# A decoder layer on one core: weight sums of the down projection made by an accumulating DMA, and one more chunk with seven products

## The chip, the core and the metric

The kernel runs on one core of one Trainium2 chip. TensorE (PE in the profile) multiplies, VectorE (DVE) and ScalarE (ACT) do elementwise work, GpSimd (POOL) little here, and SyncE (SP) issues nearly all DMAs. The time is device microseconds of one execution; the median of the runs shown is 377.06 us (376.8 to 377.14, three runs). The profile is of one more execution, which took 376.66 us; its span, from the first to the last instruction, is 374.9 us, and 1.8 us lie around it. All arithmetic is in float32. TensorE takes float32 at full pace only in a rounded form (fp32r), so each operand is split into a rounded part `hi` and a remainder `lo`, and each product is three matmuls: hi x hi, lo x hi, hi x lo.

## The reference

A decoder layer on 256 tokens of width 1024: a mixer with pooled windows and attention, a cross attention into 256 memory tokens, and a feed-forward block, each followed by a layer norm. The change touches the last product of the last block only:

```python
def swiglu(h, w_gate, w_up, w_down):
    return (jax.nn.silu(h @ w_gate) * (h @ w_up)) @ w_down
...
h = layer_norm(DEEPNORM_ALPHA * h + swiglu(h, w_gate[l], w_up[l], w_down[l]),
               ln3_g[l], ln3_b[l])
```

`w_down` is 2816 x 1024. The activations that it multiplies are 256 x 2816.

## The kernel before

**Tiles of weights.** All weights run through one `Stream`, as tiles of 128 rows and 512 KB, in the order of use. A tile goes three ways: a DMA on SyncE's queue brings it from HBM into a raw buffer, which the profile calls w103r for tile 103 (there are `RAW_BUFS` = 7 of them); ScalarE casts it to w103h; VectorE subtracts to get w103l. `prepare` issues the cast and the subtraction, up to ten tiles ahead of TensorE (`W_BUFS` + `LATE_BUFS`), and `fetch_ahead` (L112) issues loads as raw buffers come free. Each queue runs in the order in which the program wrote it, so a load that waits for a raw buffer holds back the loads behind it.

**Chunks.** The feed-forward width 2816 is cut into eleven chunks of 256. Gate and up make the activations of chunk after chunk (tiles up to w102); for each, `Gated` adds two parts of the product (L963, L964), applies the activation (L968, L969) and splits the result (L429, L430). Then down multiplies chunk by chunk, in the order `DOWN` (L38).

**Eight products, or seven.** A chunk's part of down is a 2 x 2 block matrix (128 inputs of the chunk by 512 outputs) times a 2 x 2 block matrix of activations (two token halves of 128). `eight` (L1054) does it with eight block products of 128 x 512, 24 matmuls. `seven` (L1033) does it in the Strassen-Winograd way with seven, 21 matmuls, into the eight PSUM banks m[0] to m[7]; it pays with sums of activation blocks (L977 to L984, with a second split at L984) and of weight blocks. Seven chunks, 1 to 7, go through `seven`; chunk 0 goes third through `eight`; the last three chunks (`LAST`: 8, 9, 10) go through `pieces`, which ends quarter by quarter so that the last norm can begin.

**A pair.** In `seven`, the chunk's two weight tiles are x = (x1, x2) and y = (y1, y2), each half 512 wide. `prepare_pair` (L122) makes four sums in three steps, all on VectorE, and needs a third raw buffer, z:

- step 0: z1 = x2 - x1 (L135), z2 = y2 - x2 (L136), the remainder of x1, called the corner residual (L137, tile w103c), x2 := y2 - z1 (L138), the remainder of y (L139);
- step 1: x1 := y1 - x2 (L142), the remainder of z (L143);
- step 2: the remainder of x, which now holds two sums (L146).

So a pair takes three tile numbers: 103, 104 and 105 are x, y and z of the first. ScalarE's casts (L133, L134, L141, L145) run beside. TensorE takes three products after step 0 (the corner's and two of y's tile), two after step 1 and two after step 2. Before the change tiles 103 to 108 are the first two pairs (chunks 1, 2), 109 and 110 the plain tiles of chunk 0, 111 to 125 the other five pairs, 126 to 131 the plain tiles of `LAST`. z is never loaded.

**The end.** When the pairs are through, VectorE forms the sums of the banks (u2, u3) and the residuals (L1111 to L1121), and the two token halves go through the last norm. Its power (L725) runs on GpSimd, and for the first half so does the last add (L742).

Of the kernel before, what the change touches and what calls it, by code (L numbers as in the profile page):

```python
# [11 lines left out]
OP = mybir.AluOpType  # L12
# [3 lines left out]
D = 1024  # L16
# [18 lines left out]
BUSY = 7  # L35


DOWN = (1, 2, 0, 3, 4, 5, 6, 7, 8, 9, 10)  # L38
SEVEN = (1, 2, 3, 4, 5, 6, 7)
LAST = DOWN[-3:]  # L40
ALL = slice(None)

# [3 lines left out]
def r32(t):  # L46
    return t.bitcast(F32)


class Stream:  # L50
# [38 lines left out]
    def fetch(self, upto, queue):  # L89

        while len(self.raws) < min(upto, len(self.src)):
            i = len(self.raws)
            for load in self.loads.pop(i, []):
                load()
            src = self.src[i]
            if i < len(self.homes):
                raw = self.homes[i]
            else:
                raw = self.raw_pool.tile(self.shape(i), F32, tag="raw", name=f"w{i}r")
            if src is not None:  # L100
                for s, q in self.cuts.get(i, [(slice(None), queue)]):
                    q.dma_start(raw[:, :, s], src[:, :, s])
            self.raws.append(raw)

    def shape(self, i):
# [16 lines left out]
    def prepare_pair(self, i, hi, lo):  # L122
        nc = self.nc
        first, step = self.pairs[i]
        self.fetch(first + 3, nc.sync)
        x, y, z = self.raws[first:first + 3]
        h = x.shape[2] // 2
        (x1, x2), (y1, y2), (z1, z2) = [(a[:, :, :h], a[:, :, h:]) for a in (x, y, z)]
        sub = nc.vector.tensor_sub

        if step == 0:
            own = self.corner[first] = self.own(first)
            nc.scalar.copy(own[:, 0:1, :], x1)  # L133
            nc.scalar.copy(hi, y)  # L134
            sub(z1, x2, x1)  # L135
            sub(z2, y2, x2)  # L136
            sub(own[:, 1:2, :], x1, r32(own[:, 0:1, :]))  # L137
            sub(x2, y2, z1)  # L138
            sub(lo, y, r32(hi))  # L139
        elif step == 1:  # L140
            nc.scalar.copy(hi, z)  # L141
            sub(x1, y1, x2)  # L142
            sub(lo, z, r32(hi))  # L143
        else:
            nc.scalar.copy(hi, x)  # L145
            sub(lo, x, r32(hi))  # L146
# [60 lines left out]
def decoder_layer(  # L207
# [3 lines left out]
    nc = tc.nc  # L211
# [17 lines left out]
    def accbank(name):  # L229
        return pa.tile([P, 512], F32, tag="acc", name=name)  # L230


    ws = Stream(nc, rp, wp)
# [30 lines left out]
    c_dn = {}  # L264
    for c in DOWN:
        tiles = [w_down[k * P:(k + 1) * P, :].rearrange("(k p) n -> p k n", p=P) for k in (2 * c, 2 * c + 1)]
        c_dn[c] = ws.add_pair(*tiles) if c in SEVEN else [ws.add(w, 1)[0] for w in tiles]
    ws.own = lambda i: sp.tile([P, 2, 512], F32R, tag="pair", bufs=3, name=f"w{i}c")
# [3 lines left out]
    class Both:  # L272
# [9 lines left out]
        def pair(self, k, ts=ALL):  # L282
            t, j = self.tiles[k // 4], k % 4
            return t[:, j, 0, ts], t[:, j, 1, ts]
# [17 lines left out]
    def split_xt(k, n=2):  # L302
        split(*xT.parts(k, n), xr[:, k:k + n, :])
# [7 lines left out]
    def split_mem(k):  # L311
        split(*mT.parts(k, 4), mr[0][:, k:k + 4, :])
# [46 lines left out]
    def three(ps, w, y, start, stop, part=False):  # L359

        (wa, wb), (ya, yb) = w, y
        nc.tensor.matmul(ps, wa, ya, start=start, stop=False, skip_group_check=part)  # L362
        nc.tensor.matmul(ps, wa, yb, start=False, stop=False, skip_group_check=part)  # L363
        nc.tensor.matmul(ps, wb, ya, start=False, stop=stop, skip_group_check=part)  # L364
# [63 lines left out]
    def split(h, l, ps):  # L428
        nc.scalar.copy(h, ps)  # L429
        nc.vector.tensor_sub(l, ps, r32(h))  # L430
# [5 lines left out]
    def transpose_tok(dst, tok, t, k0):  # L436

        ps = bank("tp")
        for k in range(4):
            nc.tensor.transpose(ps[:, k * P:(k + 1) * P], tok[:, (k0 + k) * P:(k0 + k + 1) * P], ident)  # L440
        ts = slice(t * P, (t + 1) * P)
        split(*dst.parts(k0, 4, ts), ps.rearrange("p (k t) -> p k t", k=4))
# [145 lines left out]
    sums = {}  # L588
# [109 lines left out]
    class Norm:  # L698
# [9 lines left out]
        def add(self, c0, c1, acc):  # L708
            self.sum(c0, c1, acc)
            self.measure(c0, c1)  # L710
# [201 lines left out]
    def gated_parts(c):  # L912


        if c in SEVEN:
            t = ap.tile([P, 2, 8, P], F32R, tag="a8", name=f"g{c}")
            gT[c] = t[:, 0], t[:, 1]
            return
        i, j = divmod([c for c in sorted(DOWN) if c not in SEVEN].index(c), 2)
        if i == 0 and j == 0:  # L920
            shared[i] = ap.tile([P, 2, 8, P], F32R, tag="a8", name=f"go{i}")
        if i == 0:
            gT[c] = tuple(shared[i][:, n, 4 * j:4 * j + 4] for n in range(2))
        elif j == 0:
            gT[c] = tuple(sp.tile([P, 4, P], F32R, name=f"go{n}", tag="pr", bufs=PR_BUFS) for n in range(2))
        else:
            t = ap.tile([P, 2, 4, P], F32R, tag="a8", name=f"go{i}")
            gT[c] = t[:, 0], t[:, 1]

    def gated_pair(c, k, t):  # L930

        return pair(gT[c], ALL, 2 * k + t)
# [18 lines left out]
    class Gated:  # L951
# [19 lines left out]
        def split(self):  # L971
            gated_parts(self.c)
            hi, lo = gT[self.c]
            q = self.sums[0].rearrange("p f (t s) -> p (f t) s", t=T)
            split(hi[:, 0:4], lo[:, 0:4], q)
            if self.c in SEVEN:
                a11, a21, a12, a22 = [q[:, i] for i in range(4)]  # L977
                sums = sp.tile([P, 4, P], F32, name="sg", tag="pr", bufs=PR_BUFS)
                s1, s2, s3, s4 = [sums[:, i] for i in range(4)]
                nc.vector.tensor_add(s1, a21, a22)  # L980
                nc.vector.tensor_sub(s3, a11, a21)
                nc.vector.tensor_sub(s2, s1, a11)
                nc.vector.tensor_sub(s4, a12, s2)  # L983
                split(hi[:, 4:8], lo[:, 4:8], sums)  # L984

    first = [bank("pg") for t in range(T)]
# [37 lines left out]
    m = {n: accbank(f"m{n}") for n in (1, 2, 3, 5)}  # L1024
# [3 lines left out]
    def into(n, y, w, cols=ALL, ps=None):  # L1028

        three((m[n] if ps is None else ps)[:, cols], y, w, n not in begun, True, True)  # L1030
        begun.add(n)

    def seven(c):  # L1033


        first = c_dn[c][0]
        plan = (((1, 0, None), (2, 2, 0), (3, 7, 1)), ((5, 4, 0), (7, 6, 1)), ((6, 5, 1), (4, 3, 0)))
        for i, products in enumerate(plan):
            ws.prepare(first + i + 1)
            hi, lo = ws.tiles[first + i]  # L1040
            for n, form, half in products:
                if half is None:
                    own = ws.corner[first]
                    w = own[:, 0], own[:, 1]
                else:
                    w = tuple(a[:, 0, half * 512:(half + 1) * 512] for a in (hi, lo))
                into(n, pair(gT[c], ALL, form), w)
                yield
            ws.used += 1
            ws.next()  # L1050

    QUARTERS = {2: (0, 0, 512), 3: (0, 512, D), 4: (1, 0, 512), 0: (1, 512, D)}

    def eight(c):  # L1054

        for k, number in enumerate(c_dn[c]):
            ws.prepare(number + 1)
            hi, lo = ws.tiles[number]
            for n, (t, c0, c1) in QUARTERS.items():
                into(n, gated_pair(c, k, t), (hi[:, 0, c0:c1], lo[:, 0, c0:c1]))  # L1060
            ws.used += 1
            ws.next()
            yield

    def pieces():


# [18 lines left out]

    def down():
        for c in DOWN[:-len(LAST)]:
            yield from (seven if c in SEVEN else eight)(c)

    dn = down()
    run(dn, 2)
    left.multiply()
# [5 lines left out]
    lower, upper = slice(0, 512), slice(512, D)  # L1099
    norms = [Norm(3, t, h2[:, t, :]) for t in range(T)]  # L1100

    def with_residual(t, s, y):
        nc.vector.scalar_tensor_tensor(norms[t].r[:, s], h2[:, t, s], ALPHA, y, op0=OP.mult, op1=OP.add)
# [4 lines left out]
    def shared_sum(name):  # L1108
        return sp.tile([P, 512], F32, name=name, tag="pr", bufs=PR_BUFS)

    m1, u2, u3 = [shared_sum(name) for name in ("m1", "u2", "u3")]  # L1111
# [3 lines left out]
    with_residual(0, upper, m[5])  # L1115
    nc.vector.tensor_add(u3, m[7], u2)
    with_residual(1, upper, m[5])
    nc.vector.tensor_add(norms[0].r[:, upper], norms[0].r[:, upper], u2)
    nc.vector.tensor_add(norms[1].r[:, upper], norms[1].r[:, upper], u3)
    with_residual(1, lower, u3)  # L1120
    add(norms[1], 768, D, m[0][:, 256:])  # L1121
    rest = [sp.tile([P, CW], F32R, name=f"rest{i}", tag="pr", bufs=PR_BUFS) for i in range(2)]
    nc.scalar.copy(rest[0], norms[1].r[:, 768:])
    dn = pieces()
# [87 lines left out]
```

## Time and profile before

| | |
|---|---|
| median of the runs | 377.06 us |
| the profiled execution, its span | 376.66 us, 374.9 us |
| TensorE, weight loads | 368.5 us (98%), 317.6 us (85%) |
| VectorE, ScalarE, GpSimd | 306.8 us (82%), 204.1 us (54%), 19.6 us (5%) |
| DMA, mean over the span | 71.93 MB, 192 GB/s |
| granted TensorE clock | 0.997 |
| down, from its first matmul to TensorE's last long wait | 312.3 to about 367 us |

In a row of a timeline the first number is the start in us from the span's start, the second the length in us, then engine, source line, operation, `out<-in` by the names of the tiles, and the number of instructions merged in the row. Matmuls overlap in the pipeline: the distance of their starts is what one costs. VectorE's instructions overlap a little as well (0.69 us long, 0.60 apart), so distances of starts are used there too. In brackets stands the idle time before an instruction and what ended it. In the list of DMA issues the last number is the time from issue to landing in us. The down stage is where tiles 103 and up are used; VectorE works on them from 288.83 us on, some 20 us ahead.

### The profile page before, as it was taken

What the parts mean: (1) busy time and instruction counts of PE and PEld (TensorE: products, weight loads), DVE (VectorE), ACT (ScalarE), POOL (GpSimd) and SP (SyncE); (2) the same over time, 40 slices, a digit from 0 to 9 for tenths busy, and PEclk for the clock granted to TensorE, in tenths of its full rate; (3) what the DMA queues carried; (4) which work ended last, traced back from release to release, by engine and by line L of the source; (5) the groups of instructions that cost most, each with busy time, mean ns of one, the idle gap of its engine ahead of it and who ended that gap; (6) DMA issues with size and microseconds to landing.
All of it is one profiled execution on the core that took longest, in us unless ns stands there. A gap on an engine that the chain in (4) does not pass through costs nothing.

```text
span 374.9 us, 5582 instructions
## 1 busy us (share of the span) xinstructions
PE 368.5 (98%) x2061; PEld 317.6 (85%) x2061; DVE 306.8 (82%) x498; ACT 204.1 (54%) x330; POOL 19.6 (5%) x27
## 2 busy tenths in 40 slices
PE   9999999999999999999999999999999999999994
PEld 8997878787888889998888888888898888888883
DVE  6768799975599677865889688888888999999984
ACT  6746677644154635644237675567665675546510
POOL 1000033400020000000100000000000000000021
PEclk9999999999999999999999999999999999999998
DMA  8997784668508963343106958665554453375202
GB/s 274 415 416 270 222 282 124 214 214 292 169 0 281 387 210 133 113 156 123 60 2 221 326 184 278 226 219 176 173 180 170 152 170 113 119 275 162 64 0 112
DMA packets 20891, 71.93 MB, mean 192 GB/s; under 512 B 2304, under 2 KB 3072, under 8 KB 20736
## 3 DMA queue, kind: packets, MB, share of 16 engines
q1 hardware_dynamic: 20432, 71.12, 54.3%
q10 hardware_dynamic: 432, 0.46, 0.4%
q8 instruction: 16, 0.26, 0.3%
q14 instruction: 11, 0.09, 0.1%
HBM read 70.52 MB, written 1.05 MB: 191 GB/s over the span
## 4 chain that ended last, share of the span: by engine, by line
PE 97%; DMA 1%; DVE 1%; ACT 0%; issue 0%; POOLq 0%; ACTq 0%
PE pg L377 19%; PE pg L383 10%; PE pqk L483 6%; PE m L362 5%; PE m L364 5%; PE m L363 5%; PE acc L362 4%; PE acc L363 4%; PE acc L364 4%; PE pxk L377 4%; PE pxq L377 4%; PE pxq L383 2%; PE pu L377 2%; PE pxk L383 2%; PE xv L362 2%; PE xv L364 2%
## 5 line engine op out<-in xcount | busy, mean ns | idle before, releaser
L725 POOL TENSOR_TENSOR rs<-rs,mhalf 128x1 f32<-128x1 f32 x6 | 5.0, 830 | 291.2 <-DVE rs L724 291.2
L429 ACT CAST g<-sg 128x512 fp32r<-128x512 f32 x14 | 8.7, 621 | 19.1 <-DVE sg L983 12.4
L430 DVE TENSOR_TENSOR g<-sg,g 128x512 fp32r<-128x512 f32 x14 | 9.7, 692 | 8.9 <-ACT g L429 8.9
L964 DVE TENSOR_TENSOR sg<-pg,sg 128x256 f32<-128x256 f32 x40 | 14.1, 416 | 0.0
L963 ACT COPY sg<-pg 128x256 f32<-128x256 f32 x40 | 11.8, 379 | 2.1 <-PE pg L383 2.1
L968 ACT ACTIVATE sg<-sg 128x512 f32<-128x512 f32 x10 | 6.3, 635 | 12.1 <-DVE sg L964 12.0
L520 ACT ACTIVATE xpr<-xs,mx 128x256 f32<-128x256 f32 x8 | 3.7, 470 | 14.3 <-DVE mx L531 14.3
L520 ACT ACTIVATE pr<-pr,mx 128x128 f32<-128x128 f32 (+1 forms) x16 | 7.1, 445 | 7.6 <-DVE mx L551 7.6
L429 ACT CAST h2T<-tp 128x512 fp32r<-128x512 f32 x4 | 2.3, 586 | 12.9 <-PE tp L440 12.9
L730 DVE SCALAR_TENSOR_TENSOR r<-r,mv,gb 128x512 f32<-128x512 f32 (+2 forms) x12 | 8.3, 722 | 0.0
L717 DVE BATCH_NORM_STATS2 st<-r 128x6 f32<-128x512 f32 (+1 forms) x12 | 8.0, 670 | 0.3
L969 DVE TENSOR_TENSOR sg<-sg 128x512 f32<-128x512 f32 x10 | 6.9, 692 | 0.8
L596 POOL TENSOR_TENSOR win<-upad 128x542 f32<-128x542 f32 x2 | 4.0, 1998 | 56.9 <-DVE upad L627 56.9
L525 DVE RECIPROCAL sm<-sm 128x2 f32<-128x2 f32 x12 | 2.0, 166 | 6.0 <-ACT xpr L520 4.5
L835 PE MATMUL xs<-xkTh,xq 128*128 128x256 f32 x32 | 6.4, 282 | 0.0
L429 ACT CAST h1T<-tp 128x512 fp32r<-128x512 f32 x4 | 2.4, 588 | 7.2 <-PE tp L440 7.2
L735 DVE SCALAR_TENSOR_TENSOR h<-r,rs,gb 128x512 f32<-128x512 f32 x8 | 5.7, 746 | 0.1
L596 POOL TENSOR_TENSOR win<-win 128x269 f32<-128x269 f32 (+3 forms) x4 | 5.8, 1446 | 0.2
L635 ACT CAST xkTh<-pxk 128x256 fp32r<-128x256 f32 x8 | 2.6, 377 | 5.5 <-PE pxk L383 5.5
L637 DVE TENSOR_TENSOR xkl<-pxk,xkTh 128x256 f32<-128x256 f32 x8 | 3.0, 416 | 3.1 <-ACT xkTh L635 3.1
L835 PEld LDWEIGHTS xs<-xkTh,xq 128*128 128x128 f32 x32 | 5.2, 190 | 0.2
L170 ACT CAST w39h<-w39r 128x1024 fp32r<-128x1024 f32 x1 | 1.0, 1049 | 7.8 <-PE acc L364 7.8
(1157 smaller groups left out, 1294.8 us busy)
## 6 DMA issues: line engine op xcount, KB each, us to landing
gb<-in_ln_g SPq DMA_DIRECT2D x3, 512.0 KB, 6.0
gb<-in_ln_b SPq DMA_DIRECT2D x3, 512.0 KB, 7.5
wr<-in_w_qkv SPq DMA_DIRECT2D x5, 256.0 KB, 4.4
mr<-in_mem_t SPq DMA_DIRECT2D x1, 1024.0 KB, 11.4
xt<-in_x SPq DMA_DIRECT2D x1, 1024.0 KB, 7.8
xr<-in_x_t SPq DMA_DIRECT2D x3, 256.0 KB, 6.1
wr<-in_w_qkv SPq DMA_DIRECT2D x1, 512.0 KB, 6.0
w7r<-in_w_qkv SPq DMA_DIRECT2D x1, 512.0 KB, 6.9
```

Source lines behind the costliest of these rows:

```text
L362: nc.tensor.matmul(ps, wa, ya, start=start, stop=False, skip_group_check=part)
L363: nc.tensor.matmul(ps, wa, yb, start=False, stop=False, skip_group_check=part)
L364: nc.tensor.matmul(ps, wb, ya, start=False, stop=stop, skip_group_check=part)
L377: nc.tensor.matmul(ps, hi[:, b * P:(b + 1) * P], yT.both(k), start=k == 0, stop=False, skip_group_check=True)
L383: nc.tensor.matmul(ps[:, S:], lo[:, b * P:(b + 1) * P], yT.pair(k)[0], start=False, stop=k == KD - 1, skip_group_check=True)
L429: nc.scalar.copy(h, ps)
L483: nc.tensor.matmul(qk[i][:, f, :], w[:, c * P:(c + 1) * P], y, start=k == 0 and f == 0 and w is hi and y is x_hi, stop=k == KD - 1 and w i ...
L520: nc.scalar.activation(dst[:, j, :], src[:, j, :], AF.Exp, bias=mx[:, j:j + 1], scale=sign, accum_out=sm[:, j:j + 1])
L596: nc.gpsimd.tensor_add(nxt[:, j:, 2 * n - 1:], cur[:, j:, 2 * n - 1:], cur[:, j:, n - 1:PADW + S - n])
L835: nc.tensor.matmul(ps[:, t, :], q[:, kk, t * P:(t + 1) * P], k[:, 2 * h + kk], start=n == 0, stop=q is q_lo and kk == 1, skip_group_check= ...
L963: nc.scalar.copy(y[:, f, :], ps[:, S:])
L964: nc.vector.tensor_add(y[:, f, :], ps[:, :S], y[:, f, :])
```

## The change

A pair's z tile is no longer computed. It is loaded: its first half gets x2, its second half y2, in two DMAs of 256 KB on SyncE's queue, and then a DMA on GpSimd's queue adds the whole of x to it on the way from HBM. So z1 = x2 + x1 and z2 = y2 + x2; the signs of the other weight sums, of two activation sums and of two adds at the end change to match. L135 and L136 go. GpSimd's DMA waits until both halves have landed; VectorE's sum x2 := y2 + z1 and ScalarE's cast of z wait for GpSimd's DMA.

The order of chunks becomes 1 to 8, 0, 9, 10. Chunk 8 now goes through `seven`, as the eighth and last pair, and chunk 0 through `pieces` in its place; `eight` is gone. Tiles 103 to 126 are the eight pairs, 127 to 132 the plain tiles. In the built program the raw buffers come round as follows: the y and the z of pair p+2 take the buffers of y and z of pair p, and the x of pair p+3 takes that of x of pair p. Their loads stand in this order on SyncE's queue: y, the two halves of z, x. The buffer of z is free after the remainder of z (line 143), that of y after line 142, that of x after step 2.

On GpSimd the eight accumulating DMAs stand between the norm of the cross attention and the last norm, with nothing else between. The order of matmuls is otherwise as before, 2058 in place of 2061.

```diff
-DOWN = (1, 2, 0, 3, 4, 5, 6, 7, 8, 9, 10)
-SEVEN = (1, 2, 3, 4, 5, 6, 7)
+DOWN = (1, 2, 3, 4, 5, 6, 7, 8, 0, 9, 10)
+SEVEN = DOWN[:-3]
...
+            sums = i in self.pairs and self.pairs[i][1] == 2
...
             if src is not None:
                 for s, q in self.cuts.get(i, [(slice(None), queue)]):
                     q.dma_start(raw[:, :, s], src[:, :, s])
+            elif sums:
+                upper, lower = self.src[i - 2:i]
+                h = upper.shape[2] // 2
+                self.nc.sync.dma_start(raw[:, :, :h], upper[:, :, h:])
+                self.nc.sync.dma_start(raw[:, :, h:], lower[:, :, h:])
+                self.nc.gpsimd.dma_start(raw, upper, accum_op=OP.add)
...
-            sub(z1, x2, x1)
-            sub(z2, y2, x2)
             sub(own[:, 1:2, :], x1, r32(own[:, 0:1, :]))
-            sub(x2, y2, z1)
+            nc.vector.tensor_add(x2, y2, z1)
...
-            sub(x1, y1, x2)
+            nc.vector.tensor_add(x1, y1, x2)
...
-                nc.vector.tensor_add(s1, a21, a22)
+                nc.vector.tensor_sub(s1, a21, a22)
...
-                nc.vector.tensor_sub(s4, a12, s2)
+                nc.vector.tensor_add(s4, a12, s2)
...
-    def eight(c):
...
-            yield from (seven if c in SEVEN else eight)(c)
+            yield from seven(c)
...
-    nc.vector.tensor_add(norms[0].r[:, upper], norms[0].r[:, upper], u2)
-    nc.vector.tensor_add(norms[1].r[:, upper], norms[1].r[:, upper], u3)
+    nc.vector.tensor_sub(norms[0].r[:, upper], norms[0].r[:, upper], u2)
+    nc.vector.tensor_sub(norms[1].r[:, upper], norms[1].r[:, upper], u3)
     with_residual(1, lower, u3)
-    add(norms[1], 768, D, m[0][:, 256:])
...
-    nc = bacc.Bacc("TRN2", target_bir_lowering=False, num_devices=1, dynamic_dma_scratch_size=256)
+    nc = bacc.Bacc("TRN2", target_bir_lowering=False, num_devices=1, dynamic_dma_scratch_size=512)
```

[...]

More of the change, by code (lines that the diff above doesn't have):

```diff
@@ L1052, in decoder_layer @@
     QUARTERS = {2: (0, 0, 512), 3: (0, 512, D), 4: (1, 0, 512), 0: (1, 512, D)}
-    def eight(c):
[L1056 to L1063, printed above, removed]
     def pieces():
```

## The prediction

> **What bounds the kernel now.** I read the page first, then the list of TensorE's waits over the whole execution, then the down stage alone: its stretches, TensorE's timeline, VectorE's timeline, and the DMA issues.
>
> ```profile
> span 374.9 us, 5582 instructions
> ...
> PE 368.5 (98%) x2061; PEld 317.6 (85%) x2061; DVE 306.8 (82%) x498; ACT 204.1 (54%) x330; POOL 19.6 (5%) x27
> ...
> PE 97%; DMA 1%; DVE 1%; ACT 0%; issue 0%; POOLq 0%; ACTq 0%
> ```
>
> ```profile
> PE end L1156 <- ACT diag L1153: 1.5, 1, 1.5
> PE busy L453 <- PEq L1175: 0.8, 1, 0.8
> PE acc L362 <- DVE xkTl L639: 0.2, 1, 0.2
> ```
>
> TensorE holds 97% of the chain that ended last and waits three times, 2.5 us in all, never in down. So time is won only by taking matmuls away, and lost only where a weight tile comes too late for TensorE. One stretch of down (330 to 335 us; the columns are length, busy time and count of PE, PEld, DVE, ACT, POOL, then clock, DMA share, GB/s) and TensorE's timeline there:
>
> ```profile
> 330.00:335.00 5.00, 5.00 (x23) 4.13 (x22) 4.94 (x7) 2.85 (x4) 0.00 (x0) 1.00 0.86 307
> ```
>
> ```profile
> 312.31 0.40 PE L362 MATMUL m<-w103c,g 128*128 128x512 f32 x1
> ...
> 321.86 0.39 PE L362 MATMUL m<-w109h,go 128*128 128x512 f32 x1
> ...
> 327.30 0.39 PE L362 MATMUL m<-w111c,g 128*128 128x512 f32 x1
> ...
> 332.06 0.39 PE L362 MATMUL m<-w114c,g 128*128 128x512 f32 x1
> ...
> 349.97 0.39 PE L363 MATMUL m<-w125l,g 128*128 128x512 f32 x1
> ```
>
> A chunk with seven products takes 332.06 - 327.30 = 4.76 us for 21 matmuls, 0.2267 each. The one chunk with eight takes 327.30 - 321.86 = 5.44 us for 24, the same pace. VectorE, which makes the tiles, is full as well (4.94 of 5.00) and slower:
>
> ```profile
> 320.15 0.69 DVE L135 TENSOR_TENSOR w116r<-w114r 128x512 f32<-128x512 f32 x1
> ...
> 326.71 0.68 DVE L135 TENSOR_TENSOR w119r<-w117r 128x512 f32<-128x512 f32 x1
> 327.31 0.69 DVE L136 TENSOR_TENSOR w119r<-w118r,w117r 128x512 f32<-128x512 f32 x1
> 327.92 0.68 DVE L137 TENSOR_TENSOR w117c<-w117r,w117c 128x512 fp32r<-128x512 f32 x1
> 328.52 0.68 DVE L138 TENSOR_TENSOR w117r<-w118r,w119r 128x512 f32<-128x512 f32 x1
> 329.12 1.22 DVE L139 TENSOR_TENSOR w117l<-w118r,w117h 128x1024 fp32r<-128x1024 f32 x1
> 330.25 0.69 DVE L142 TENSOR_TENSOR w117r<-w118r,w117r 128x512 f32<-128x512 f32 x1
> 330.86 1.22 DVE L143 TENSOR_TENSOR w118l<-w119r,w118h 128x1024 fp32r<-128x1024 f32 x1
> 332.13 1.23 DVE L146 TENSOR_TENSOR w119l<-w117r,w119h 128x1024 fp32r<-128x1024 f32 x1
> 333.28 0.68 DVE L135 TENSOR_TENSOR w122r<-w120r 128x512 f32<-128x512 f32 x1
> ...
> 345.39 1.23 DVE L146 TENSOR_TENSOR w125l<-w123r,w125h 128x1024 fp32r<-128x1024 f32 x1
> ```
>
> A pair costs VectorE 333.28 - 326.71 = 6.57 us against TensorE's 4.76, so its lead shrinks by 1.8 us a pair. At the last pair it is 349.97 - (345.39 + 1.23) = 3.35 us, and that still covers everything.
>
> **The change, part by part.** *Matmuls.* Chunk 8 goes through seven products and chunk 0 moves into the last group, which keeps its three chunks: one chunk of 24 becomes 21. 3 x 0.2267 = **0.68 us off TensorE's path**, the only term that can shorten it.
>
> *VectorE, pairs.* L135 and L136 go: 327.92 - 326.71 = 1.20 us a pair, so 5.37 is left. This shortens nothing by itself (TensorE never waits for it); it pays for the eighth pair. The remaining sums only change sign.
>
> *VectorE, chunk 8's activations* need the second split that chunk 7 had and chunk 8 had not:
>
> ```profile
> 284.43 0.69 DVE L430 TENSOR_TENSOR g<-sg,g 128x512 fp32r<-128x512 f32 x1
> ...
> 287.68 1.22 DVE L172 TENSOR_TENSOR w102l<-w102r,w102h 128x1024 fp32r<-128x1024 f32 x1 [0.26 <-ACT w102h L170]
> ...
> 297.64 0.68 DVE L430 TENSOR_TENSOR go<-sg,go 128x512 fp32r<-128x512 f32 x1
> 298.24 0.69 DVE L135 TENSOR_TENSOR w108r<-w106r 128x512 f32<-128x512 f32 x1
> ```
>
> 3.25 us (284.43 to 287.68) replaces 0.60 (297.64 to 298.24): 2.65 more. Before w114 VectorE had made three pairs and two plain tiles, 3 x 6.57 + 2 x 1.14 = 21.99 us; now it makes four pairs and the split, 4 x 5.37 + 2.65 = 24.13. So the fifth pair begins at 320.15 + 2.14 = 322.3, where TensorE wants it from 312.31 + 4 x 4.76 = 331.4. That is covered by over 7 us.
>
> *The end of down.* The 256-wide add into the second token half goes (L1121). VectorE waits for TensorE at the very next add, so it is worth nothing:
>
> ```profile
> 358.78 1.37 DVE L1106 TENSOR_TENSOR r<-m,r 128x512 f32<-128x512 f32 x2 [0.23 <-PE m L364]
> ```
>
> *The DMAs.* Each pair now loads four pieces by SyncE (two tiles, two halves of the sum tile) and one accumulating tile by GpSimd, which waits for both halves. Behind it on GpSimd stand only the other seven and the last norm's power, which ran at 362.12, some 20 us after the last sum is needed. On SyncE the two extra issues cost 327.20 - 326.82 = 0.38 us each and delay loads that are used a pair later.
>
> ```profile
> 326.82 0.33 SPq L102 DMA_DIRECT2D w124r<-in_w_down  x1
> 327.20 1.39 SPq L327 DMA_DIRECT2D gb<-in_ln_g  x1
> ```
>
> ```profile
> 362.12 0.92 POOL L725 TENSOR_TENSOR rs<-rs,mhalf 128x1 f32<-128x1 f32 x1 [170.69 <-DVE rs L724]
> ```
>
> *The new wait, the term that decides.* The sum tile of pair p+2 lies in the buffer of pair p's, free when L143 of pair p ends. Call **a** the time from there until the accumulated sum is ready. VectorE then still has step 2 of pair p (1.27 with its gap, 330.86 + 1.14 to 333.28), all of pair p+1 (5.37) and one corner residual (0.60): 7.24 us. Beyond that it stands still, and after the sum it needs 0.60 + 1.14 + 0.60 + 1.14 = 3.48 to the next L143, 4.75 to the end of the pair. Pairs 1 to 3 are loaded long before. Counting from the fifth pair's start, L143 of pair 4 ends at 322.3 - 1.27 = 321.0. Between the L143 of pairs 3 and 4 also stands chunk 10's gate work:
>
> ```profile
> 313.62 1.41 DVE L964 TENSOR_TENSOR sg<-pg,sg 128x256 f32<-128x256 f32 x4
> ...
> 316.68 0.69 DVE L969 TENSOR_TENSOR sg<-sg 128x512 f32<-128x512 f32 x1
> ...
> 319.00 1.23 DVE L146 TENSOR_TENSOR w113l<-w111r,w113h 128x1024 fp32r<-128x1024 f32 x1 [0.26 <-ACT w113h L145]
> ```
>
> That is 1.41 + (319.00 - 316.68) = 3.73, so L143 of pair 3 ends at 321.0 - 5.37 - 3.73 = 311.9. Then:
> - pair 5: sum at 311.9 + a, wanted at 322.9; late if a is over 11.0, which still costs pair 8 nothing;
> - pair 6: sum at 321.0 + a, wanted at 328.3; late by a - 7.3; it ends at 325.8 + a;
> - pair 7: sum at 326.4 + a, wanted at 326.4 + a; just in time;
> - pair 8: sum from L143 of pair 6, 324.5 + a, plus a; its first tile is ready 1.8 later, at 326.3 + 2a. TensorE wants it at 312.31 + 7 x 4.76 + 0.68 = 346.3.
>
> So nothing is lost up to **a = 10.0**. Past that it is 2 us for each us of a. From about 11.5 it is 3, an estimate by the same count: pair 4's sum hangs on L143 of pair 2, some 8.2 before pair 3's (5.37 and chunk 9's gate work, 2.8 by the pieces above), so it comes at 303.7 + a and is wanted at 311.9 + 1.27 + 1.41 + 0.60 = 315.2; what it is late passes on to pairs 6 and 8. The six plain tiles that follow take VectorE 1.14 us each and TensorE 1.36, so they lose no more.
>
> What is a? No accumulating DMA and no queue fed by GpSimd stands in the trace; its main queue is of the hardware kind:
>
> ```profile
> q1 hardware_dynamic: 20432, 71.12, 54.3%
> ```
>
> ```profile
> w103r<-in_w_down SPq DMA_DIRECT2D x1, 512.0 KB, 5.8
> ...
> w111r<-in_w_down SPq DMA_DIRECT2D x1, 512.0 KB, 3.1
> w120r<-in_w_down SPq DMA_DIRECT2D x1, 512.0 KB, 3.5
> ...
> mr<-in_mem_t SPq DMA_DIRECT2D x1, 1024.0 KB, 11.4
> ...
> out<-r SPq DMA_DIRECT2D x1, 512.0 KB, 2.6
> ```
>
> The halves: 0.38 for the second issue and 3.5 to land (w120r), 3.9 together. The accumulate, from below: a plain load of its size, 3.1, so a = 7.0 and the full 0.68 gained (no reason lets it gain more: only matmuls shorten the path). From above: a load of twice the size in full traffic, 11.4 (mr), so a = 15.3: 2 x 5.3 + 3.8 = 14.4 lost, net +13.7. Between them: it loads 512 KB, and it reads 512 KB out of SBUF, as the store of out does (2.6). With a load of 3.5 that is 6.1, with one in company (5.8, and it will have company: the next pair's first tile is issued just then) 8.4. I take the middle, 7.3: **a = 11.2**, 2 x 1.2 = 2.4 lost, less 0.68: **+1.7 us**.
>
> [...]
>
> **Result.** The profiled execution took 376.66 us with a span of 374.9; the median of the runs is 377.06. 377.06 + 1.7 = **378.8 us**.
>
> **The rivals.**
> - *The sums come in time* (a up to 10). Then only the three matmuls count: 377.06 - 0.68 = 376.4. For it: the plain load in quiet traffic, 3.1 to 3.5, leaves the accumulate 6.1 us before anything is lost. Against it: that is just the least I get when the tile's second read is counted.
> - *The DMA engines become the bound*, with the accumulate at a fraction of a plain load's rate. In the stretch above they moved 307 GB/s at a share of 0.86, so about 357 when full. A pair now moves 3 x 0.524 + 0.524 = 2.10 MB, 2.62 with the destination read: 5.9 to 7.3 us, over TensorE's 4.76. Queues then stand behind each other, a reaches 13 or more: 2 x 3 + 1.5 = 7.5 lost, +6.8, 383.9 and above. For it: the share of 0.86 already. Against it: other stretches are far emptier, and the first three pairs come early.
>
> **How the numbers follow.** Late by some (a of 10 to 13): 0.45, forecast 378.8. In time: 0.40, 376.4. DMA-bound: 0.15, 383.9 or more. About 0.2% (0.75 us) can be told from no change here. The 0.68 us of the second case lies just inside that, so it is split, 0.22 faster and 0.18 same; 0.03 of the late case (a up to 10.7) is also within. The rest, 0.57, is slower. The range runs from 376.2 (in time, and 0.2 for the runs' spread) to 386 (a = 13.7: 7.4 + 2.2 - 0.68 = +8.9). The forecast's own range is 376.4 to 383.9.
>
> **What would show it.** Right: no L135 and L136 rows; TensorE still at 0.227 a matmul; in down a VectorE wait for a DMA at the sum that takes L138's place, longest at the sixth and eighth pair; a TensorE wait on the eighth pair's first tile of about 2.4 us. Wrong: TensorE without a wait in down (in time), or waits from the fourth pair on and a DMA share near 0.9 from 310 us (DMA-bound). A landing of the accumulating DMA under 6.1 us would overturn the forecast; TensorE's pace changing would overturn the whole sum.

## The result, and the profile after

The changed kernel takes 401.27 us (400.5 to 402.01, five runs), the kernel before 377.06 in runs beside it: a ratio of 1.064 (1.0622 to 1.066), 24.2 us slower. The forecast was 378.8, the range ended at 386. The profiled execution took 401.56 us with a span of 399.8.

The head of the page of the kernel after, its engines, the granted clock in 40 slices, the queue of the accumulating DMAs, and the chain that ended last:

```profile
span 399.8 us, 5659 instructions
...
PE 376.0 (94%) x2058; PEld 321.1 (80%) x2058; DVE 302.7 (76%) x492; ACT 206.2 (52%) x333; POOL 26.9 (7%) x35
...
PEclk9999999999999999999999999999999779998898
...
q0 software_dynamic: 1152, 4.19, 5.8%
...
PE pg L382 17%; PE pg L388 9%; PE pqk L488 6%; PE acc L367 4%; PE acc L368 4%; PE acc L369 4%; DMA w126r<-in_w_down 4%; PE pxq L382 4%; PE pxk L382 4%; DMA w120r<-in_w_down 2%; PE pxq L388 2%; PE pu L382 2%; PE pxk L388 2%; PE xv L367 2%; PE xv L369 2%
```

Three matmuls are gone, as the diff says (2061 to 2058), yet TensorE is busy 376.0 us and not 368.5. VectorE is busy 4.1 us less. The chain that ended last now holds two accumulating DMAs, w120r and w126r. What TensorE and VectorE waited for (us in total, times, longest):

```profile
PE m L368 <- DVE w124l L144: 7.9, 1, 7.9
PE m L367 <- DVE sg L969: 6.4, 2, 3.9
PE m L368 <- DVE w118l L144: 1.8, 1, 1.8
...
PE m L368 <- DVE w121l L144: 0.6, 1, 0.6
```

```profile
DVE g L435 <- ACT g L434: 16.7, 15, 7.1
DVE w124r L143 <- DMA w126r<-in_w_down: 7.9, 1, 7.9
DVE w118r L143 <- DMA w120r<-in_w_down: 7.0, 1, 7.0
```

Before, TensorE had no wait in down. Now it waits 7.9 + 6.4 + 1.8 + 0.6 = 16.7 us there. That is nearly all of the 17.4 us by which its idle time grew (399.8 - 376.0 = 23.8 against 374.9 - 368.5 = 6.4). It is also busy 376.0 - 368.5 = 7.5 us longer, or 8.2 longer than the remaining matmuls took before (368.5 - 0.68). 17.4 + 7.5 = 24.9 is the difference of the spans (399.8 - 374.9). Three things stand in these rows.

**The activations' buffer.** In the timelines of ScalarE and VectorE (start, length, and in brackets the idle time before and what ended it):

```profile
306.95 0.62 ACT L434 CAST g<-sg 128x512 fp32r<-128x512 f32 x1 [7.69 <-PE pg L388]
```

```profile
307.60 0.69 DVE L435 TENSOR_TENSOR g<-sg,g 128x512 fp32r<-128x512 f32 x1 [7.09 <-ACT g L434]
```

This is the split of chunk 8's activations. As a chunk of `seven` it gets a tile of eight blocks. In the built program it lies in the buffer of the first half of h2T, the input of gate and up, and TensorE's products of gate and up (`pg`) read that half until 306.9. ScalarE's cast waits 7.7 us for them, VectorE 7.1 for the cast. Behind it in VectorE's queue stand the next gate's sums, and the PSUM banks of down's first products are free only after those:

```profile
316.42 0.77 PE L367 MATMUL m<-w103c,g 128*128 128x512 f32 x1 [3.93 <-DVE sg L969]
...
324.39 0.50 PE L367 MATMUL m<-w104h,g 128*128 128x512 f32 x1 [2.51 <-DVE sg L969]
```

Down begins at 316.4 and not at 312.3. Before, only chunk 10 took this buffer, for its smaller tile, and as the last of all.

**The accumulating DMA.** From the chain of waits, in order of time (start, length, what); left out are VectorE's work on tiles 118 and 119 and pieces of issue:

```profile
339.97 8.25 DMA w120r<-in_w_down
...
350.67 1.15 DVE w119l L148
...
351.83 0.33 SPq L107
...
352.21 6.12 DMA w126r<-in_w_down
...
359.00 8.64 DMA w126r<-in_w_down
...
367.67 0.69 DVE w124r L143
```

Here a, the time from the freeing of z's buffer to the finished sum, can be read off: 351.82 (the end of L148 of pair 6, w119l) to 367.64 is 15.8 us. Of these, 0.4 pass until the second half is issued, 6.1 until it has landed, 0.7 until GpSimd's DMA starts, 8.6 until that has landed. The same chain has the accumulate of w114r, the fourth pair, further up: every second pair hangs on the one two before it. SyncE's queue issues in the order written: it stood 8.9 us for the buffer of w125r, and the loads behind, w126r's halves and gb's, left from 351.83 us on.

**The clock.** Windows of two us, with TensorE's busy time, its matmuls, the granted clock, the DMA share and GB/s:

```profile
316.00:318.00 2.00, 1.58 (x4) 0.50 0.76 226
...
326.00:328.00 2.00, 2.00 (x6) 0.50 1.04 240
...
363.00:365.00 2.00, 0.00 (x0) 1.00 1.08 291
365.00:367.00 2.00, 0.00 (x0) 0.91 1.03 274
367.00:369.00 2.00, 0.00 (x0) 0.50 0.40 160
369.00:371.00 2.00, 1.45 (x4) 0.50 0.00 0
371.00:373.00 2.00, 2.00 (x6) 0.50 0.92 295
373.00:375.00 2.00, 2.00 (x9) 0.89 0.72 229
375.00:377.00 2.00, 2.00 (x11) 1.00 0.00 0
```

In the wait of 7.9 us the clock falls to 0.50, and it comes back some 4 us after TensorE's restart. Six matmuls run in a window instead of nine to eleven. The first wait, of 3.9 us, did the same (0.50 from 315.4 to 322.2). The second, of 2.5 us, did so as well, but only from 325.7 to 329.1, when TensorE had been running again for 1.3 us. The one of 1.8 us near 350 left the clock at 1.00. In windows of 0.2 us the six changes of the clock can be placed at 315.42, 322.25, 325.66, 329.08, 366.62 and 373.45 us: each lies a whole multiple of 3.41 us behind the first. So when the clock falls does not follow from the length of the wait alone.

Behind the three waits 29 matmuls start about 0.43 us apart and not 0.23. That is some 6 us of TensorE's 8.2 us of extra busy time: slower matmuls, not more of them. The other 2 us were not traced.

### The profile page after: what moved, and what is told of

Same layout as the page of the kernel before. It is cut to its first block, busy times and chain, and to the rows that moved or that the text cites. A ratio compares the mean times of both kernels' runs of the same rounds, so it can differ in the third digit from the quotient of the medians.

```text
span 399.8 us, 5659 instructions
## 1 busy us (share of the span) xinstructions
PE 376.0 (94%) x2058; PEld 321.1 (80%) x2058; DVE 302.7 (76%) x492; ACT 206.2 (52%) x333; POOL 26.9 (7%) x35
## 4 chain that ended last, share of the span: by engine, by line
PE 82%; DMA 8%; DVE 5%; issue 2%; ACT 1%; POOLq 0%; SPq 0%; DVEq 0%; ACTq 0%
PE pg L382 17%; PE pg L388 9%; PE pqk L488 6%; PE acc L367 4%; PE acc L368 4%; PE acc L369 4%; DMA w126r<-in_w_down 4%; PE pxq L382 4%; PE pxk L382 4%; DMA w120r<-in_w_down 2%; PE pxq L388 2%; PE pu L382 2%; PE pxk L388 2%; PE xv L367 2%; PE xv L369 2%
## 5 line engine op out<-in xcount | busy, mean ns | idle before, releaser
L434 ACT CAST g<-sg 128x512 fp32r<-128x512 f32 x16 | 9.9, 620 | 28.5 <-DVE sg L988 14.1
L435 DVE TENSOR_TENSOR g<-sg,g 128x512 fp32r<-128x512 f32 x16 | 11.1, 693 | 16.7 <-ACT g L434 16.7
L973 ACT ACTIVATE sg<-sg 128x512 f32<-128x512 f32 x10 | 6.4, 637 | 11.5 <-DVE sg L969 11.5
L368 PE MATMUL m<-w124l,g 128*128 128x512 f32 x2 | 1.4, 711 | 7.9 <-DVE w124l L144 7.9
L109 POOL DMA_DIRECT2D w105r<-in_w_down x1 | 1.1, 1058 | 94.1 <-DVE sg L985 94.1
```

## The experiments

Each is given against the kernel of before, which took 376.8 to 377.1 us in these runs. The first of them, with chunk 10 as the eighth pair, is called the first run.

**Chunk 10 as the eighth pair.** The tile that takes h2T's buffer is then chunk 10's. It has eight blocks too, but it is written when gate and up are through:

```diff
-DOWN = (1, 2, 3, 4, 5, 6, 7, 8, 0, 9, 10)
+DOWN = (1, 2, 3, 4, 5, 6, 7, 10, 0, 8, 9)
```

> The changed kernel with one edit: chunk 10 instead of chunk 8 goes through seven products, so that the activations with eight blocks are written into the buffer of h2T only after gate and up are through. Theory: the changed kernel's 24 us are two losses, each with a slow clock behind it: (A) ScalarE and VectorE stand still for 7 us at 300 us, because the activations of chunk 8 take a buffer that TensorE still reads; (B) the sums of pairs 6 to 8 come late, a = 12.6 to 15.8 us instead of 11.2. Then the wait of the cast at line 434 vanishes, TensorE starts down at 312.3 without a wait, and 390 to 395 us are left. Rival 1, the accumulating DMAs alone set the end: 399 to 402. Rival 2, the buffer wait alone: 376 to 379.

395.95 us (392.9 to 396.65), 5.3 less than the change and 19.1 more than before, just above the theory's 390 to 395. Down's first tile is no longer late. TensorE's waits are now w118l 6.8 and w124l 7.7: the 7 us of the buffer were partly in the shade of the accumulating DMAs, which now set the end alone.

**The accumulating DMA with the chunks of before** (seven pairs, chunk 0 third through `eight`).

> The accumulating DMA alone: seven pairs, chunk 0 through eight products in third place and the last group as in the kernel before. No chunk needs the buffer of h2T early. Theory: one chain link (about 8.5 us) less than with eight pairs and 5.4 us of TensorE's work in between, so the last sums still come late: 380 to 388 us. Rival (the eighth chunk is what costs): 376.5 to 378.

384.04 us (382.32 to 386.8), a ratio of 1.019 (1.0146 to 1.024): the first part of the change costs 7.2 us by itself. In the profile, of the execution that took 386.8, TensorE waits 1.4 us for the last pair's w123l and 3.3 us for the sums of the last gate (`sg`). VectorE makes these behind its own wait of 3.6 us for the third pair's sum, so a late sum also holds up work that has nothing to do with the weights.

**The eighth chunk without any accumulating DMA**, in the order of the change; VectorE adds z1 = x2 + x1 and z2 = y2 + x2:

```diff
-            elif sums:
+            elif sums and (i - 103) // 3 in ():
...
+            nc.vector.tensor_add(z1, x2, x1)
+            nc.vector.tensor_add(z2, y2, x2)
```

> The eighth chunk alone, in the changed kernel's order, with all four sums of a pair on VectorE again (the signs stay positive). Theory: the 7 us standstill at 300 us is there without any accumulating DMA, VectorE has 6.57 us a pair and no slack, so TensorE loses about as much and runs slow for a while after it: 386 to 393 us. Rival (the standstill is a matter of the DMAs, or is covered): 376 to 381.

390.84 us, 1.037 (1.0353 to 1.0391): the second part costs 14.0 by itself. TensorE's only waits in down are the two for the gate's sums, 8.8 us together. The two parts together cost 3 us more than their sum (24.2 against 7.2 + 14.0). The eighth pair adds a link to the chain of late sums, which neither part has alone; what makes up the 3 us was not separated.

**Chunk 10 as the eighth, no accumulating DMA**: the order of the first run with the adds of the third.

> The eighth chunk alone, chunk 10 in place of 8, all four weight sums made by VectorE, no accumulating DMA: neither the wait for the old buffer nor that for the sums is left. Theory: what the change's second part is worth, three matmuls less, 376.4; up to 378.5 if VectorE's eight pairs at 6.57 us use up its lead. Rival (an eighth chunk through seven products costs by itself, its second split and its sums): 380 or more.

380.43 us, 1.0086 (1.0071 to 1.0101): 10.4 less than with chunk 8, so the buffer was the reason there. But 3.3 are left, and the rival holds: the eighth chunk costs even so. VectorE's timeline of this kernel shows how (first and last rows of its seventh pair, and the first of the eighth):

```profile
340.05 0.68 DVE L143 TENSOR_TENSOR w123r<-w121r 128x512 f32<-128x512 f32 x1
...
345.47 1.23 DVE L154 TENSOR_TENSOR w123l<-w121r,w123h 128x1024 fp32r<-128x1024 f32 x1
346.74 0.69 DVE L143 TENSOR_TENSOR w126r<-w124r 128x512 f32<-128x512 f32 x1
```

```profile
PE m L371 <- DVE w124l L147: 0.8, 1, 0.8
```

VectorE takes 6.69 us for this pair without a gap, TensorE 4.76, so VectorE's lead shrinks by 1.9 a pair. In the kernel before, chunk 0 in third place let it recover (two plain tiles of 1.14 us for 24 matmuls of TensorE), and the seventh and last pair was still 3.35 us early. With eight pairs in a row the lead is gone at the seventh, and TensorE runs at VectorE's pace from there: two pairs, 3.7 us.

**The eighth chunk with the sums left out of the last four pairs**, to see whether VectorE's time is all that is missing. y's buffer stands in for z there:

```diff
+            if sums and (i - 103) // 3 in (4, 5, 6, 7):
+                self.raws.append(self.raws[i - 1])
+                continue
...
+            if (first - 103) // 3 not in (4, 5, 6, 7):
                 nc.vector.tensor_add(z1, x2, x1)
                 nc.vector.tensor_add(z2, y2, x2)
```

> Chunk 10 as the eighth, VectorE's adds for the first four pairs; in the last four the two sums of z are left out altogether, and y's buffer stands in for z (so these pairs' products are not the reference's): nobody makes the sums, and nobody waits for them. Theory (the eighth chunk cost 3.3 us because VectorE at 6.57 us a pair ran out of its lead in the last two pairs): four pairs at 5.37 cover it, no wait in down, 376.4 to 377.2: the most that taking the sums off VectorE can bring here. Rival (the eighth chunk costs by something else, its activations or its place at the end): 379.5 or more.

376.43 us, a ratio of 0.9985 (0.9976 to 0.9995), 0.57 us faster, with no wait of TensorE in down. That is the most which this change can bring: the three matmuls, worked out at 0.68.

**The second step as a plain load.** The first run's kernel without the addition (z gets x alone); all waits and all loaded bytes stay:

```diff
-                self.nc.gpsimd.dma_start(raw, upper, accum_op=OP.add)
+                self.nc.gpsimd.dma_start(raw, upper)
```

> As the run with chunk 10, but GpSimd's DMA only copies x over the sum tile and adds nothing, so the weight sums are wrong; every load, wait and issue stays. Theory: adding is what doubles the DMA's engine time (the accumulating queue took 5.8% of 16 engines for 4.19 MB, 2.9 us each, where a plain 512 KB takes 1.47); without it a falls by 2 to 4 us and the time to 380 to 388 us. Rival (the second hop, not the adding, makes the sums late): within 2 us of the run with chunk 10.

388.29 us, 1.030 (1.0277 to 1.0322): 7.7 less than with the addition, just above the theory's 380 to 388. Times from issue to landing of GpSimd's DMAs, first as in the first run, then plain (tile, queue, KB, us):

```profile
w114r<-in_w_down POOLq DMA_DIRECT2D x1, 512.0 KB, 7.5
w117r<-in_w_down POOLq DMA_DIRECT2D x1, 512.0 KB, 5.3
w120r<-in_w_down POOLq DMA_DIRECT2D x1, 512.0 KB, 9.2
...
w126r<-in_w_down POOLq DMA_DIRECT2D x1, 512.0 KB, 8.5
```

```profile
w114r<-in_w_down POOLq DMA_DIRECT2D x1, 512.0 KB, 3.7
w117r<-in_w_down POOLq DMA_DIRECT2D x1, 512.0 KB, 3.4
w120r<-in_w_down POOLq DMA_DIRECT2D x1, 512.0 KB, 6.6
...
w126r<-in_w_down POOLq DMA_DIRECT2D x1, 512.0 KB, 7.2
```

With the addition each landing shown is 1.3 to 3.8 us longer. VectorE's last wait, for w126r, is still 7.6 us without it (7.8 with it): loading in two steps is late by itself.

**Nine raw buffers**, so that z of pair p+3, and not of pair p+2, takes the buffer of z of pair p (one split tile fewer ahead pays for it):

```diff
-RAW_BUFS, W_BUFS, LATE_BUFS = 7, 8, 2
+RAW_BUFS, W_BUFS, LATE_BUFS = 7, 8, 1
...
+    ws.extra = ctx.enter_context(tc.tile_pool(name="extra", bufs=2))
...
+    def is_extra(self, i):
+        return i >= 103 and (i - 103) % 9 < 2
```

> The kernel of the run with chunk 10 as the eighth, with nine raw buffers for down's pairs and not seven (paid for by one pair of split tiles fewer, 9 ahead of TensorE and not 10): z of pair p+3, not of pair p+2, takes the buffer of z of pair p. Theory (each sum hangs on the one two pairs ahead by a, 15.4 us, and a pair of TensorE takes 4.76): with three pairs to cover a, the chain through every second pair is gone and most of the 19 us with it, 378 to 385. Rival (the DMA engines are full with the accumulating traffic, whatever the buffers): 391 or more.

381.59 us at the median (381.07 to 386.2), within the theory's 378 to 385: 14 us of the first run's 19 hung on the ring of seven. The profile is of the execution that took 386.2 (the others took 381.07 to 381.7). In it one long wait of VectorE is left, 8.5 us for w123r, which landed after 10.8 us, in a stretch where the DMA engines are nearly full. The window up to there, with TensorE's busy time, clock, DMA share and GB/s:

```profile
300.00:345.00 45.00, 42.54 (x207) 1.00 0.92 267
```

So the rival names what may come next: 0.92 of the engines' time moves 267 GB/s. No run here takes that traffic away.

**TensorE kept busy.** 24 matmuls of no use ahead of the eighth pair, into the idle bank m[0]:

```diff
+            if i == 0 and c in (10,):
+                for _ in range(24):
+                    g = gT[c][0]
+                    nc.tensor.matmul(m[0], g[:, 0], g[:, 0:4], start=True, stop=True, skip_group_check=True)
```

> The kernel of the run with chunk 10 as the eighth, with 24 matmuls of no use (5.4 us, into the idle bank m[0]) ahead of the eighth pair's first product, so that TensorE idles about 2 us there and not 7.7. Theory (the clock falls because TensorE stood still): the granted clock stays at 1.00 behind the wait, the 11 matmuls that took 0.427 us each take 0.227; VectorE's remainders then set the pace of that pair, so 1.8 us come back: 394.1 (393.4 to 394.8). Rival (the clock falls for another reason, the DMA traffic for one): half clock behind the wait as before, within 0.5 of 395.9. Slower than 397 would mean that the matmuls themselves are in the way.

393.25 us (392.79 to 393.45), 2.7 less. Windows in and behind the wait, first run and this one:

```profile
358.00:360.00 2.00, 0.00 (x0) 0.57 1.07 276
...
362.00:364.00 2.00, 0.18 (x1) 0.50 0.21 84
364.00:366.00 2.00, 2.00 (x5) 0.50 0.26 78
```

```profile
358.00:360.00 2.00, 2.00 (x11) 1.00 1.03 274
...
362.00:364.00 2.00, 1.42 (x6) 1.00 0.00 0
364.00:366.00 2.00, 1.91 (x9) 1.00 0.86 264
```

From 358 to 360 us the DMA traffic is as heavy (a share of 1.03 against 1.07), and the clock stays at 1.00: it falls because TensorE stands still. From the first product of w124l to the first of w127h it is 4.39 us (362.58 to 366.97) instead of 6.17 (363.82 to 369.99), 1.8 less as expected. The profiled execution's tile was also ready 1.2 earlier, which this run does not explain. Of TensorE's waits in down, those of 0.6 and 1.8 us in the changed kernel and of 1.7 us here left the clock at 1.00; those of 2.5, 3.9 and 7.9 us in the changed kernel and of 6.8 and 7.7 us in the first run each brought 0.50.

**Accumulating DMAs where there is time**: for the second to fourth pair only, with seven raw buffers, and for the fifth and seventh only, with nine.

> The kernel of the run with chunk 10 as the eighth, with the accumulating DMA for the second to fourth pair only (issued from 285 to 305 us, when VectorE is 20 us ahead), and VectorE's adds for the other five. Theory (an accumulating DMA costs only where its landing, 15 us behind the freeing of its buffer, comes too late): 376.0 to 378. Rival (its traffic or GpSimd's queue costs wherever it runs): 380 or more.

> Nine raw buffers, chunk 10 as the eighth, and the accumulating DMA for the fifth and seventh pair only; VectorE's adds for the other six. Theory (with the eighth chunk VectorE's 6.57 us a pair against TensorE's 4.76 use up its lead of ten tiles, which costs 3.7 us in the last two pairs; a sum taken off VectorE pays only behind the point where the ring of split tiles holds VectorE up, and only if it lands in time): 2 x 1.20 us come back from the 380.4 of the kernel with VectorE's adds, less up to 1.6 for one split tile fewer ahead: 378 to 379.8. Rival (the late accumulating DMAs land too late even with three pairs to cover them): 381 or more.

The early ones give 380.33 us at the median, the same as VectorE's adds (380.43), so by the number the rival holds. Of the 3 x 1.20 = 3.6 us taken off VectorE, 1.5 go into a wait for w114r and 0.7 into one for ScalarE's copy of the gate's products: between 310 and 325 us VectorE stands idle 3.6 us, where it stood 1.4 with its own adds. The other 1.2 are kept: it begins the fifth pair at 325.68 us and not at 326.92. In the profiled execution (379.63) TensorE then waits 1.0 us in down and not 1.8; the other three took 380.3 and more, so nothing of this shows in them. The late two give 383.25, and the rival holds: w117r came in time, w123r took 9.7 us to land and held VectorE up for 4.0. Nine buffers with VectorE's adds alone were not run, so the price of the one split tile fewer is not separated.

**GpSimd's adds instead**, two of 128x512 on GpSimd, for all eight pairs and for the last four:

```diff
-                self.nc.sync.dma_start(raw[:, :, :h], upper[:, :, h:])
-                self.nc.sync.dma_start(raw[:, :, h:], lower[:, :, h:])
-                self.nc.gpsimd.dma_start(raw, upper, accum_op=OP.add)
+                self.nc.gpsimd.tensor_add(raw[:, :, :h], x[:, :, h:], x[:, :, :h])
+                self.nc.gpsimd.tensor_add(raw[:, :, h:], y[:, :, h:], x[:, :, h:])
```

> Chunk 10 as the eighth, and the two sums of z made by GpSimd, in two adds of 128x512 (1.3 us each by the last norm's add in the profile of before), issued where the change issues its DMAs; nothing is added on the way from HBM. Theory (the change lost by the time from the freeing of z's buffer to the finished sum, 15 us, not by taking the sums off VectorE): that time is about 3 us, no wait in down, VectorE at 5.37 us a pair keeps its lead, only the three matmuls count: 376.4 (376.0 to 377.2). Rival (taking the sums off VectorE gains nothing, or GpSimd's adds slow VectorE's): 380 or more.

> As the run with GpSimd's adds, for the last four pairs only; VectorE's adds for the first four. Theory (what is saved on VectorE counts only behind the point, near 322 us, where the ring of split tiles last holds it up; 4 x 1.20 us cover the 3.7 that were lost): 376.4 to 377.2, the same as with GpSimd in all eight pairs. Rival (GpSimd's adds cost VectorE time wherever they run, so fewer are better): faster than with all eight by 0.5 or more.

383.94 us with all, 382.73 with the last four; with none it was 380.43. Both expectations of 376.4 failed, the rival holds. Timelines of the first, VectorE and then GpSimd:

```profile
335.10 1.23 DVE L150 TENSOR_TENSOR w117l<-w115r,w117h 128x1024 fp32r<-128x1024 f32 x1
336.25 1.79 DVE L141 TENSOR_TENSOR w118c<-w118r,w118c 128x512 fp32r<-128x512 f32 x1
337.96 1.78 DVE L142 TENSOR_TENSOR w118r<-w119r,w120r 128x512 f32<-128x512 f32 x1
```

```profile
335.13 2.36 POOL L107 TENSOR_TENSOR w123r<-w121r 128x512 f32<-128x512 f32 x1 [3.50 <-DVE w116l L147]
337.47 1.72 POOL L108 TENSOR_TENSOR w123r<-w122r,w121r 128x512 f32<-128x512 f32 x1
```

VectorE's operations of 0.69 us take up to 1.79 beside GpSimd's. While the last three sums are made, two of them do: 2 x 1.1 = 2.2 us lost to save 1.20; earlier it is mostly one. GpSimd's take 2.36 and 1.72 instead of 1.3. The lengths fit engines that take turns: GpSimd's first add, which starts under a VectorE operation, would be held until that ends at 336.3, and VectorE's next until GpSimd's ends at 337.5. What holds them was not shown.

Only the run that leaves sums out was faster than the kernel before, by 0.57 us; every other version was slower.

## Why the prediction was right or wrong

- **Three matmuls, -0.68:** right, 0.57 measured (0.2 to 0.9) once everything else is out of the way. Their pace is that of the rounded form: in the trace of before a plain float32 product of 128x256 (`pm`, L607) takes two instructions whose starts lie 0.22 us or more apart, a rounded one of that size (`pqk`, L483) one every 0.12 us.
- **VectorE 6.57 to 5.37 a pair:** right (L135 and L136 are gone), and so was what it is for: "it pays for the eighth pair". Without it 3.3 us are lost, with the sums simply gone nothing is.
- **Chunk 8's second split, "covered by over 7 us":** the step that failed first. Its 2.65 us were costed as work, and the cover was there. What was not asked is where its output goes: a larger tile, in a buffer that gate and up still read. ScalarE's cast waited 7.7 us for that place. It cost 10.4 us of the time without accumulating DMAs (390.84 against 380.43) and 5.3 with them (401.27 against 395.95).
- **Loss through pairs 4, 6 and 8, each hanging on the one two before:** right. The chain of waits names w114r, w120r and w126r, and a third generation of buffers took 14 us away. "Pairs 1 to 3 are loaded long before" does not hold for the first: VectorE waited 3.9 us for w105r. It was far ahead of TensorE there, and no wait of TensorE follows at that place.
- **The size of a, 11.2:** the deciding term was mis-sized; at the eighth pair it was 15.8, past the upper bound of 15.3. The halves took 6.5 and not 3.9. They had the company of gb's loads, of w125r's and w127r's and of the end of the accumulate before, with the engines' share at 0.93 to 1.09 from 352 to 358 us; no run takes these away one by one. The accumulate took 8.6 and not 7.3. 0.7 us until GpSimd's DMA started were not counted. A landing under 6.1 us was named as what would overturn the forecast: four of the eight accumulates took 5.1 to 5.3 us (pairs 2, 3, 5 and 7), but the ones that pairs 4, 6 and 8 waited for took 7.3 to 8.6.
- **The rival with full DMA engines** had the better number (a of 13 and more), at 0.15, and its signs: VectorE waited from the fourth pair on (2.6 us for w114r), and the engines' share was 0.86 from 331 to 369 us. Eight accumulates took 5.8% of 399.8 us of all engines, 2.9 us each, against 1.5 for the same bytes as a plain load (3.1% of 386.7 in that run). With three loads of 512 KB beside it that is 3 x 1.5 + 2.9 = 7.4 us a pair, the upper end that it gave (7.3). The read of the tile in SBUF, which the sum and this rival count, was the author's estimate: the runs show the 2.9 against 1.5, not the read itself. But full engines were not the first limit: with nine buffers the same traffic cost 14 us less.
- **The loss per us of a:** by the prediction's count, 2(11.5 - 10) + 3(15.4 - 11.5) = 14.7 us of waiting for the first run's a of 15.4 at its sixth and eighth pair. TensorE's two waits there are 6.8 + 7.7 = 14.5, so the count was good for this value of a. Less the 0.68 it gives +14.0, against 19.1 measured. 1.8 of the difference are the clock behind the second wait. Behind the first, eight matmuls start 0.43 us apart as well, an estimate of 1.6 more; the other 1.7 were not separated. For the changed kernel, with its a of 15.8, the count gives 377.06 + 15.2 = 392.3 us: the size of a alone does not make 401.27.
- **The clock:** no step had it, though "TensorE's pace changing" was named as what would overturn the sum. It is a price on top of each wait of 2.5 us or more in these runs: the sum took TensorE's 4.76 us a pair as given behind a stall.

## What to carry to other kernels

When work moves to another place in an order, ask for each tile which it writes whose buffer it gets and who reads that last: the rows of the engine that does the work say nothing about it. A DMA that adds took twice a plain load's share of the engines here (2.9 against 1.5 us for 512 KB), and a two-step load begins only when its buffer is free, so its latency (15.8 us at the eighth pair) counts once per turn of the ring of buffers. What an engine saves is worth something only if it reaches the place where its lead is used up: taken off earlier, 2.2 of 3.6 us went into VectorE's other waits here.

## What the runs showed of the hardware that was not expected

- The granted clock fell to 0.50 inside a kernel that is busy 94% of the time, after single waits of 2.5 us and more, and each time slow matmuls followed for 3 to 6 us. In the changed kernel's profile its changes lie whole multiples of 3.41 us apart.
- An accumulating DMA of 512 KB from HBM into SBUF took 5.0 to 10.8 us from issue to landing in these runs, against 3.4 to 7.2 for a plain one from the same queue. In the windows from 363 to 367 us above, under w126r's accumulate, a DMA share of 1.03 to 1.08 moved only 274 to 291 GB/s; from 361 to 363 us, under the same accumulate, a share of 1.04 moved 420. Which transfers make the difference was not traced.
- Two GpSimd adds cost VectorE more time (2.2 us a pair, for the last three pairs) than its own two (1.20).
